# A group's projections moved ahead of the scans as seven half products each, and two scans woven beside the output projection

## The chip, the cores and the metric

The kernel runs on one core of a Trainium2 chip. The metric is the device time of one execution in microseconds (us), the median of three runs.

## The reference, cut to what matters

The trunk has two layers, a selective state space (SSD) layer and a pooling layer. 1,024 prompt tokens and 64 sample tokens (8 sequences of 8) go through it together, 1,088 columns in all. Only the first layer is touched here:

```python
zxbcdt = h @ w_in                       # h: normed, modulated x (1024 features)
z, xbc, dt_raw = ...                    # z: 2048, x: 2048, B, C: 8 groups of 128 each
conv = conv_b + sum(xp[:, k:k+L] * conv_w[k] for k in range(4))
xbc_act = silu(conv)                    # x, B and C of each of 8 groups
y, new_ssm = ssd_scan(xs, dt, A, B, C, ssm_prev)   # chunks of 128 tokens, state carried along
gated = (y + D * xs) * silu(z)          # then normed within each group of 256 channels
out = (gated * norm_g) @ w_out          # 2048 -> 1024, the output projection
x = x + (1 + gate) * out
```

The eight groups are independent until the output projection, which sums over all 2,048 gated channels.

## The kernel before, in words

All data are float32, and each number is split into a high and a low part so that a product takes three matrix multiplications (high by high, high by low, low by high: L168 to L170 in one helper, L922 to L924 in the other). TensorE (PE) does nearly all of the work; VectorE (DVE), ScalarE (ACT) and GpSimd (POOL) make the parts, evacuate the sums from PSUM and do the scans' elementwise work; SyncE (SP) issues the DMAs.

The first layer goes through these stages:

- **Front** (up to about 270 us): norm, modulation, and then eight *pairs* of weight tiles, named in the table `FRONT`. A pair computes two 128-column tiles of the projection at once by a scheme of seven half products in place of eight (`fast_pair`): products B11, B21, T2, T3, T1, T4, B22, each of 24 matmuls of 272 columns. Each product takes one or two PSUM buffers by tag, in the order mm mm, tr tr, y y, mm S, mm mm, tr tr, y y; there are two buffers of tags tr and y, so T4 can start only when B21's sums have been added up by DVE (`put`, L933), and B22 only when T2's have been. A pair of kind z gives two tiles of z, which go to DRAM. A pair ("b", g) gives B and C of group g and ("x", g) its two x tiles. These four tiles then pass the convolution, `conv_tile`: ACT L332, three DVE steps L334, ACT L337 (the sigmoid's half), DVE L338 and L340. The sums before the convolution and its accumulator lie in buffers called `raw`, of which there are three.
- **Scans** (about 270 to 791 us): for g from 0 to 6 the scan of group g is woven beside the four projection tiles of group g+1 (`proj_group`: four weight tiles of 72 matmuls of 364 or 360 columns, each followed by its convolution). `weave` takes one step of the scan and then some steps of the other work.
- **Transition and scan 7** (791 to 876 us): scan 7 has no projection left to stand beside, and is woven with part 0 of the output projection. That projection is done in four parts of four k (512 of the 2,048 gated channels); a part has 24 units of 12 matmuls. For each k, `op_stage` loads the gated tile `gr` from DRAM (and the norm factors `rs` for each two k), and `op_split` multiplies the two (DVE L679) and splits the result into `gh` (ACT L683) and `gl` (DVE L684). k = 0 to 3 are needed for part 0.
- **Rest of the output projection** (876 to about 1,030 us): the parts that are left, with the splits of the next part paced among their units (`op_paced`), then the pooling layer.

The order in which an engine gets its instructions is fixed when the kernel is built, by the order of the code and the buffers' priorities. An engine does its instructions in that order, and one that waits holds up all those behind it.

Of the kernel before, what the change touches and what calls it, by code (L numbers as in the profile page):

```python
# [7 lines left out]
F32 = mybir.dt.float32  # L8
# [6 lines left out]
P = 128  # L15
# [14 lines left out]
AE = 1  # L30
# [5 lines left out]
NSLOT_E = 4  # L36
FRONT = (("z", 2), ("z", 3), ("z", 4), ("z", 5), ("b", 0), ("z", 6), ("x", 0), ("z", 7))
WIDE = 1223
# [11 lines left out]
class Slots:  # L50
# [11 lines left out]
    def add_extra(self, pool, n):  # L62
        self.e = [f"e{i}" for i in range(n)]
        self.pools.update({t: (pool, TOK) for t in self.e})

    def get(self, name, dtype=F32, wide=False, short=False, extra=False):
        older = short and self.a and self.b and self.freed.get(self.b[0], 0) <= self.freed.get(self.a[0], 0)
        tag = (self.e if extra and self.e else self.b if self.b and (wide or older or not self.a) else self.a).pop(0)
        pool, w = self.pools[tag]
        self.n += 1  # L70
        t = pool.tile([P, w], dtype, tag=tag, name=f"{name}_{self.n}")
        v = t if wide else t[:, :TOK]
        self.used[id(v)] = (tag, v)
        return v

    def free(self, *ts):
        for t in ts:
            tag = self.used.pop(id(t))[0]
            {"s": self.a, "t": self.b, "e": self.e}[tag[0]].append(tag)
            self.count += 1  # L80
            self.freed[tag] = self.count


class Build:
    def __init__(self, tc, io):
        self.tc, self.nc, self.io = tc, tc.nc, io
        self.uid = 0

# [253 lines left out]
    def raw_tile(self):  # L342
        return self.gp.tile([P, 1115], F32, tag="raw", bufs=3, name=self.name("raw"))

# [119 lines left out]
    def scan_group(self, g, T):  # L464
# [160 lines left out]
        for c in range(8):  # L625
            Fn = front(c + 1)
            if c == 7:
                self.slots.free(B)
            back(c, F)
            F = Fn  # L630
            if c == 5:
                load_h0()
            if c == 6:
                load_z()
            if c == 7:
                zsc = sample_inter()
                self.slots.free(C)
            yield
        nc.sync.dma_start(self.io["hpT"][g], h.rearrange("p r q -> p (r q)"))
# [26 lines left out]
    def op_stage(self, src, k, short=False, rsd=None):  # L666

        if rsd and k % 2 == 0:
            self.rst = self.slots.get("rs", short=short)
            self.nc.sync.dma_start(self.rst, rsd[k // 2].rearrange("j n -> (j n)").unsqueeze(0).to_broadcast([P, TOK]))  # L670
        raw = self.slots.get("gr", short=short)
        self.nc.sync.dma_start(raw, src[k])
        return k, raw, self.rst if rsd else None
# [365 lines left out]
    def run(self):  # L1039
# [7 lines left out]
        items += [(io["win"][6 * g + {"b": 0, "x": 2, "z": 4}[kind] + i], 0) for kind, g in FRONT for i in range(2)]  # L1047
        for g in range(1, 8):
            for ii in range(4):
                items.append((io["win"][6 * g + ii], 8))  # L1050
                if (g, ii) in self.ada_plan:
                    items += self.ada_items(self.ada_plan[g, ii])
# [12 lines left out]
        with tc.tile_pool(name="cp", bufs=1) as self.cp, tc.tile_pool(name="wp", bufs=1) as self.wp, \  # L1065
# [7 lines left out]
            self.rsd = [dr.tile([4, 272], F32, tag=f"rsd{i}", name=f"rsd{i}") for i in range(8)]  # L1073
            self.zsd = [dr.tile([P, TOK], F32, tag=f"zsd{i}", name=f"zsd{i}") for i in range(16)]
            self.b12d = [dr.tile([P, HALF], F32, tag=f"b12d{i}", name=f"b12d{i}") for i in range(8)]
            self.x1d = [dr.tile([P, TOK], F32, tag=f"x1d{i}", name=f"x1d{i}") for i in range(8)]
            with tc.tile_pool(name="gp", bufs=1) as self.gp:
                with tc.tile_pool(name="ga", bufs=1) as self.tp:
                    self.slots.add_extra(self.tp, NSLOT_E)
                    self.setup()  # L1080
                    self.front()
                with tc.tile_pool(name="gs", bufs=1) as self.gs:
                    self.ssd_layer()
            with tc.tile_pool(name="gp2", bufs=1) as self.gp2:
# [135 lines left out]
    def front_pairs(self, ops, dt):  # L1220

        nc, sl = self.nc, self.slots
        self.fast_init(len(FRONT))
        G = None
        for n, (kind, g) in enumerate(FRONT):
# [3 lines left out]
            else:  # L1229
                G = G or self.proj_open(g)  # L1230
                ii = 2 * (kind == "x")
# [3 lines left out]
            def after(x):  # L1235
# [11 lines left out]
                if kind != "z" and x == "B22":  # L1247
                    for i in range(2):
                        self.proj_end(G, ii + i, ts[i])
                if n == 0 and x in ("B11", "B21"):  # L1250
                    next(ops)
# [11 lines left out]
        sl.free(*[self.T[4, k] for k in range(4)])  # L1263
        self.G = G

    def ssd_layer(self):
        nc, sl = self.nc, self.slots
        T, sc = self.G["out"], ()
        for g in range(7):
            G = self.proj_open(g + 1)  # L1270
            sc, pr = self.scan_group(g, T), self.late(self.proj_group(G), 1, sc)
            T = G["out"]
            if g < 6:
                self.weave(itertools.islice(sc, 11), pr, (1, 1, 1, 1, 1, 1, 1, 1, 1, 1, 2))
# [6 lines left out]
        for _ in itertools.chain(sc, pr):  # L1281
            pass
        for a in self.ada_late[:AE]:
            for _ in self.ada_do(a):
                pass
# [6 lines left out]
        for d in range(XA):  # L1292
            self.load_x(d)
        sc, fill = self.scan_group(7, T), self.op_units(0, acts, self.ada_late[AE:])
        self.weave(itertools.islice(sc, 10), fill, (1, 2, 2, 2, 2, 2, 2, 2, 2, 2), False)

        self.nxt = [split(stage(k)) for k in (4, 5)]
        self.weave(sc, fill, (2, 2, 2))
        self.free_acts(acts)

# [7 lines left out]
    def weave(self, main, fill, counts, drain=True):  # L1308

        i, md, fd = 0, False, False  # L1310
        while not (md and fd):
            if not md:
                md = next(main, 0) == 0
            if md and not drain:
                return
            for _ in range(99 if md else counts[min(i, len(counts) - 1)]):
                fd = fd or next(fill, 0) == 0
# [8 lines left out]

    def op_paced(self, l, acts, nxt):

        next(nxt)
        for i, ins in enumerate(self.op_units(l, acts)):  # L1330
            if i % 3 == 2:
# [20 lines left out]
    def ssd_out(self):  # L1352
        nc, sl, x = self.nc, self.slots, self.x
        sg = self.vec[:, V_SG:V_SG + 16]
        acts = self.nxt
        for _ in self.op_part_load(self.gyd, sg, (6, 8), acts, False, self.rsd):
            pass
        for i in (2, 3):
            nxt = []
            self.op_paced(0, acts, self.op_part_load(self.gyd, sg, PARTS[i], nxt, i == 3, self.rsd))  # L1360
            self.free_acts(acts)
            acts = nxt
        ss, rst = sl.get("ss"), sl.get("rst")
# [198 lines left out]
```

## Time and profile before

| what | us |
|---|---|
| median of three runs | 1685.69 |
| fastest and slowest of them | 1685.56, 1687.11 |
| time of the profiled execution | 1685.18 |
| its span, from first to last instruction | 1683.4 |
| PE busy within the span | 1649.9 |

The profiled execution is 0.5 us under the median, and 1.8 us of its time lie around the span. PE is busy for 98% of the span, DVE for 76%, ACT for 47%, POOL for 26%. "Busy" holds a matmul at half clock for as busy as one at full clock, so the granted clock has to be read beside it. Times below are counted from the start of the span.

### The profile page before, as it was taken

How to read it: one execution, taken by the hardware profiler on the slowest of the kernel's cores; microseconds unless marked ns; L12 is line 12 of the kernel's file. 1: busy time of each engine (PE TensorE's matmuls, PEld its weight loads, DVE VectorE, ACT ScalarE, POOL GpSimd, SP SyncE). 2: the span in 40 equal slices, each digit the busy share in tenths (PEclk: the TensorE clock that was granted, in tenths of full speed). 3: DMA queues.
4: the chain of work that ended last, by engine and by line, in shares of the span. 5: the costliest groups of instructions: out<-in, count | busy, mean ns of one | idle time of the engine just before them, and what ended most of it. 6: DMA issues, size and time to landing. Idle time of an engine off the chain costs nothing.

```text
span 1683.4 us, 30188 instructions
## 1 busy us (share of the span) xinstructions
PE 1649.9 (98%) x11771; PEld 1556.7 (92%) x11771; DVE 1274.0 (76%) x2182; ACT 785.5 (47%) x1539; POOL 446.0 (26%) x467
## 2 busy tenths in 40 slices
PE   8999999999999999999999999999999999999997
PEld 6899999889898888888889998999999999999997
DVE  6897688777778778788787647999999876555545
ACT  6544336767657676767442227533332343122123
POOL 0134440313122231222010022376666620000012
PEclk9999999999999999999999999999999999999998
DMA  8422225445354544445875132132333467411102
GB/s 336 164 89 104 78 80 207 146 145 182 108 171 121 167 127 141 141 123 182 285 247 192 43 116 79 67 125 97 111 110 110 138 250 305 155 52 51 38 26 106
DMA packets 111246, 232.03 MB, mean 138 GB/s; under 512 B 16864, under 2 KB 56960, under 8 KB 111104
## 3 DMA queue, kind: packets, MB, share of 16 engines
q1 hardware_dynamic: 111104, 230.10, 40.2%
q8 instruction: 93, 1.52, 0.4%
q14 instruction: 49, 0.40, 0.1%
HBM read 172.09 MB, written 57.98 MB: 137 GB/s over the span
## 4 chain that ended last, share of the span: by engine, by line
PE 34%; POOL 8%; issue 8%; DVE 5%; DMA 1%; ACT 1%; POOLq 0%; SPq 0%; ACTq 0%; DVEq 0%
PE mm L168 9%; PE mm L169 9%; PE mm L170 9%; POOL w L162 2%; PE st L924 1%; PE st L923 1%; PE st L922 1%; POOL sw L888 1%; POOL sw L887 1%; POOL npl L777 1%; POOL wr L892 1%; POOL npl L778 1%; DVE gl L684 1%; POOL sw L894 1%; PE y L550 0%
## 5 line engine op out<-in xcount | busy, mean ns | idle before, releaser
L168 PE MATMUL mm<-gh,wh 128*128 128x364 f32 (+3 forms) x768 | 254.8, 333 | 1.7 <-DVE x L703 1.3
L169 PE MATMUL mm<-gl,wh 128*128 128x364 f32 (+3 forms) x768 | 254.0, 331 | 2.2 <-DVE gl L684 2.2
L170 PE MATMUL mm<-gh,wl 128*128 128x364 f32 (+3 forms) x768 | 253.7, 331 | 0.0
L168 PE MATMUL mm<-hh,wh 128*128 128x364 f32 x720 | 248.4, 345 | 0.0
L169 PE MATMUL mm<-hl,wh 128*128 128x364 f32 x720 | 239.0, 332 | 0.0
L170 PE MATMUL mm<-hh,wl 128*128 128x364 f32 x720 | 237.6, 330 | 0.0
L703 DVE SCALAR_TENSOR_TENSOR x<-mm,gat,x 128x364 f32<-128x364 f32 (+3 forms) x192 | 108.9, 571 | 148.3 <-PE mm L170 147.9
L924 PE MATMUL st<-hh,w 128*128 128x272 f32 x704 | 203.2, 289 | 0.8 <-DVE w L162 0.8
L923 PE MATMUL st<-hl,w 128*128 128x272 f32 x704 | 203.1, 288 | 0.0
L922 PE MATMUL st<-hh,w 128*128 128x272 f32 x704 | 202.9, 288 | 0.0
L125 ACT ACTIVATE wh<-wr 128x1024 fp32r<-128x1024 f32 x73 | 77.2, 1057 | 224.6 <-PE mm L169 209.1
L924 PE MATMUL st<-t,w 128*128 128x272 f32 x528 | 152.4, 289 | 3.8 <-POOL w L162 2.9
L923 PE MATMUL st<-t,w 128*128 128x272 f32 x528 | 152.2, 288 | 0.7 <-DVE t L1190 0.7
L922 PE MATMUL st<-t,w 128*128 128x272 f32 x528 | 151.7, 287 | 0.0
L168 PEld LDWEIGHTS mm<-gh,wh 128*128 128x128 f32 x768 | 144.8, 189 | 5.4 <-DVE x L703 2.0
L169 PEld LDWEIGHTS mm<-gl,wh 128*128 128x128 f32 x768 | 145.4, 189 | 3.8 <-DVE gl L684 2.8
L170 PEld LDWEIGHTS mm<-gh,wl 128*128 128x128 f32 x768 | 145.5, 189 | 0.3 <-issue 0.2
L563 POOL TENSOR_TENSOR hd<-h,cd 128x256 f32<-128x256 f32 x56 | 67.1, 1198 | 282.4 <-DVE h L564 139.4
L334 DVE SCALAR_TENSOR_TENSOR raw<-raw,cwh,raw 128x1112 f32<-128x1112 f32 x96 | 134.3, 1399 | 9.8 <-ACT raw L332 9.1
L168 PEld LDWEIGHTS mm<-hh,wh 128*128 128x128 f32 x720 | 135.4, 188 | 5.5 <-ACT raw L376 1.6
L169 PEld LDWEIGHTS mm<-hl,wh 128*128 128x128 f32 x720 | 135.5, 188 | 4.6 <-issue 3.0
L170 PEld LDWEIGHTS mm<-hh,wl 128*128 128x128 f32 x720 | 135.3, 188 | 3.0 <-issue 2.9
(267 smaller groups left out, 4060.7 us busy)
## 6 DMA issues: line engine op xcount, KB each, us to landing
wr<-win SPq DMA_DIRECT2D x48, 512.0 KB, 4.8
acb<-acd SPq DMA_DIRECT2D x64, 256.0 KB, 3.9
wr<-pin SPq DMA_DIRECT2D x32, 512.0 KB, 3.6
x<-xT SPq DMA_DIRECT2D x16, 544.0 KB, 7.3
zsd<-z SPq DMA_DIRECT2D x16, 544.0 KB, 2.7
z<-zsd SPq DMA_DIRECT2D x16, 544.0 KB, 5.8
gyd<-xbc SPq DMA_DIRECT2D x16, 544.0 KB, 4.9
gr<-gyd SPq DMA_DIRECT2D x16, 544.0 KB, 4.9
```

What stands on the lines that cost most here:

```text
L125: self.nc.scalar.activation(hi[:, :nk, :], raw[:, :nk, :], AF.Copy)
L162: eng.tensor_tensor(out=lo, in0=src, in1=hi.bitcast(F32), op=ALU.subtract)
L168: nc.tensor.matmul(ps[:, :n], hi[:, k, :], ah[:, a:a + n], start=first, stop=False)
L169: nc.tensor.matmul(ps[:, :n], hi[:, k, :], al[:, a:a + n], start=False, stop=False)
L170: nc.tensor.matmul(ps[:, :n], lo[:, k, :], ah[:, a:a + n], start=False, stop=last)
L334: nc.vector.scalar_tensor_tensor(out=acc[:, :n], in0=raw[:, k:k + n], scalar=w[k], in1=acc[:, :n], op0=ALU.mult, op1=ALU.add)
L563: nc.gpsimd.tensor_tensor(out=hd, in0=h, in1=cd.unsqueeze(2).to_broadcast([P, 4, 64]), op=ALU.mult)
L684: nc.vector.scalar_tensor_tensor(out=lo, in0=raw, scalar=scl[:, k:k + 1], in1=hi.bitcast(F32), op0=ALU.mult, op1=ALU.subtract)
L703: ins = nc.vector.scalar_tensor_tensor(out=x[d][:, a:a + pn], in0=ps[:, :pn], scalar=self.gat[l][:, d, 8:9], in1=x[d][:, a:a + pn], op0=AL ...
L922: nc.tensor.matmul(ps[c][:, :QUART], hi[:, k], xh[:, t], start=(k == 0), stop=False)
L923: nc.tensor.matmul(ps[c][:, :QUART], hi[:, k], xl[:, t], start=False, stop=False)
L924: nc.tensor.matmul(ps[c][:, :QUART], lo[:, k], xh[:, t], start=False, stop=(k == 3))
```

## The change

Group 7's B, C and x are projected in the front, as two more pairs of seven half products, `("b", 7)` and `("x", 7)`. Their four tiles go through the convolution there, are stored to DRAM (`xbd`) and loaded again for scan 7. Scans 0 to 5 stand beside the projections of groups 1 to 6 as before; scans 6 and 7 follow each other (`last_scans`) beside two and a half parts of the output projection (`ssd_parts`), two units after a scan step and three after the next, in turn. The `raw` buffers get tags of their own, r0 to r2, and after the last convolution they are lent to `gr` and `rs`. Loading z within a scan moves from step 5 or 6 to step 7. Lines move by 4 in the part up to 1,000: L334 becomes L338, L338 and L340 become L342 and L344, L679 and L684 become L683 and L688, L933 becomes L937, L162 becomes L166.

```diff
-FRONT = (("z", 2), ("z", 3), ("z", 4), ("z", 5), ("b", 0), ("z", 6), ("x", 0), ("z", 7))
+FRONT = (("z", 2), ("z", 3), ("z", 4), ("b", 7), ("z", 5), ("x", 7), ("b", 0), ("z", 6), ("x", 0), ("z", 7))
...
+    def add_raw(self, pool):
+        self.e = [f"r{i}" for i in range(3)]
+        self.pools.update({t: (pool, 1115) for t in self.e})
...
     def raw_tile(self):
-        return self.gp.tile([P, 1115], F32, tag="raw", bufs=3, name=self.name("raw"))
+        self.nraw += 1
+        return self.gp.tile([P, 1115], F32, tag=f"r{self.nraw % 3}", name=self.name("raw"))
...
-            self.rst = self.slots.get("rs", short=short)
+            self.rst = self.slots.get("rs", short=short, extra=True)
...
-        raw = self.slots.get("gr", short=short)
+        raw = self.slots.get("gr", short=short, extra=True)
...
-        for g in range(1, 8):
+        for g in range(1, 7):
             for ii in range(4):
                 items.append((io["win"][6 * g + ii], 8))
...
                     for i in range(2):
                         self.proj_end(G, ii + i, ts[i])
+                        if g:
+                            nc.sync.dma_start(self.xbd[ii + i], G["out"][ii + i])
+                            sl.free(G["out"][ii + i])
...
-        for g in range(7):
+        for g in range(6):
             G = self.proj_open(g + 1)
             sc, pr = self.scan_group(g, T), self.late(self.proj_group(G), 1, sc)
...
+        sl.add_raw(self.gp)
...
-        sc, fill = self.scan_group(7, T), self.op_units(0, acts, self.ada_late[AE:])
-        self.weave(itertools.islice(sc, 10), fill, (1, 2, 2, 2, 2, 2, 2, 2, 2, 2), False)
-
-        self.nxt = [split(stage(k)) for k in (4, 5)]
-        self.weave(sc, fill, (2, 2, 2))
-        self.free_acts(acts)
+        self.fill = self.ssd_parts(acts)
+        self.weave(self.last_scans(T), self.fill, (2, 3), False)
+        assert len(sl.e) == 3
+
+    def last_scans(self, T):
+
+        yield from self.scan_group(6, T)
+        T = [self.slots.get("xbc") for _ in range(4)]
+        for i, t in enumerate(T):
+            self.nc.sync.dma_start(t, self.xbd[i])
+        yield from self.scan_group(7, T)
+        self.scanned = True
+
+    def ssd_parts(self, acts):
+
+        sg = self.vec[:, V_SG:V_SG + 16]
+        self.scanned = False
+        for p in range(3):
+            nxt = []
+            ld = self.op_part_load(self.gyd, sg, PARTS[p + 1], nxt, p == 2, self.rsd)
+            yield from self.op_paced(0, acts, ld, (11, 2, 13)[p], self.ada_late[AE:] if p == 0 else (), p == 2)
+            self.free_acts(acts)
+            acts = nxt
+        self.nxt = acts
```

The first place at which the order matters is DVE's queue behind the last convolutions ahead of a pair. Before, pair z6 follows b0: `raw_2154` and `raw_2157` are the tiles of b0, `raw_2392` and `raw_2403` the accumulators of their convolutions, and the puts of z6 write `z_2413` and `z_2414`.

```order
L334 SCALAR_TENSOR_TENSOR raw_2392<-raw_2154,cwh,raw_2392 128x1112 x2
L162 TENSOR_TENSOR w_2449<-sw_2291,w_2449 128x512
L334 SCALAR_TENSOR_TENSOR raw_2392<-raw_2154,cwh,raw_2392 128x1112
L933 TENSOR_TENSOR z_2413<-st_2452,u_2415 128x272
L933 TENSOR_TENSOR z_2413<-st_2453,u_2415 128x272
L933 TENSOR_TENSOR u_2415<-st_2489,u_2415 128x272
L338 SCALAR_TENSOR_TENSOR xbc_2391<-raw_2154,raw_2392 128x1024
L340 SCALAR_TENSOR_TENSOR xbc_2391<-raw_2154,raw_2392 128x64
```

In the changed kernel pair b0 follows x7. `raw_2419` and `raw_2422` are the tiles of x7, `raw_2657` and `raw_2669` their accumulators, and the first put of b0 writes `raw_2684`.

```order
L338 SCALAR_TENSOR_TENSOR raw_2657<-raw_2419,cwh,raw_2657 128x1112
L342 SCALAR_TENSOR_TENSOR xbc_2656<-raw_2419,raw_2657 128x1024
L344 SCALAR_TENSOR_TENSOR xbc_2656<-raw_2419,raw_2657 128x64
L166 TENSOR_TENSOR w_2788<-sw_2556,w_2788 128x512
L338 SCALAR_TENSOR_TENSOR raw_2669<-raw_2422,cwh,raw_2669 128x1112 x2
L166 TENSOR_TENSOR w_2824<-wr_2554,w_2824 128x512
L338 SCALAR_TENSOR_TENSOR raw_2669<-raw_2422,cwh,raw_2669 128x1112
L166 TENSOR_TENSOR w_2858<-wr_2554,w_2858 128x512
L342 SCALAR_TENSOR_TENSOR xbc_2668<-raw_2422,raw_2669 128x1024
L344 SCALAR_TENSOR_TENSOR xbc_2668<-raw_2422,raw_2669 128x64
L937 TENSOR_TENSOR raw_2684<-st_2727,u_2690 128x272
L937 TENSOR_TENSOR raw_2684<-st_2728,u_2690 128x272
```

The puts of the next pair stood between the steps of the convolutions before; now the first of them (of product B21) stands behind both convolutions, since b0's tiles take up `raw` buffers that these still use.

The second place is SP's queue at the transition. Before, the loads of `gr` for k = 2 and 3 (`gr_9324`, `gr_9326`) stand ahead of the last scan's state output and of the first x tiles.

```order
L661 DMA gyd_86<-xbc_8410 128x1088
L672 DMA gr_9324<-gyd_75 128x1088
L109 DMA wr_9375<-adaA 128x1024
L672 DMA gr_9326<-gyd_76 128x1088
L619 DMA hsT<-h_129_8919 128x1024
L1325 DMA x_9338<-xT 128x1088
```

In the changed kernel the same two loads (`gr_9007`, `gr_9009`) stand behind the factors' output `rsd_126`, the x tiles and the first weights of the output projection.

```order
L663 DMA rsd_126<-z_8768 4x272
L368 DMA ncT<-ncv_8107 128x108
L1355 DMA x_9024<-xT 128x1088
L1355 DMA x_9025<-xT 128x1088
L113 DMA wr_9060<-adaA 128x1024
L107 DMA wr_9062<-wout 128x2x512
L1355 DMA x_9022<-xT 128x1088
L676 DMA gr_9007<-gyd_75 128x1088
L676 DMA gr_9009<-gyd_76 128x1088
```

They go into two of the lent `raw` buffers, those of the last convolution, so they wait for its last DVE step (L344) where before they went into buffers that were free earlier.

## Rows read from the trace of the kernel before

**Rows 1.** The page's busy times, and the granted clock in 40 slices.

```profile
PE 1649.9 (98%) x11771; PEld 1556.7 (92%) x11771; DVE 1274.0 (76%) x2182; ACT 785.5 (47%) x1539; POOL 446.0 (26%) x467
...
PEclk9999999999999999999999999999999999999998
```

**Rows 2.** Windows by stage: scans 5 and 6, transition, scan 7, plain projection.

```profile
core 0: us, PE busy (x) PEld busy (x) DVE busy (x) ACT busy (x) POOL busy (x), PEclk, DMA share, GB/s
...
640.00:714.00 74.00, 73.22 (x530) 65.46 (x529) 58.20 (x97) 50.84 (x113) 18.19 (x27) 1.00 0.39 120
714.00:791.50 77.50, 76.71 (x549) 67.19 (x547) 63.73 (x101) 54.37 (x117) 18.66 (x27) 1.00 0.46 147
791.50:810.00 18.50, 15.08 (x81) 11.99 (x81) 15.60 (x20) 9.72 (x13) 0.33 (x2) 0.72 0.82 298
810.00:876.40 66.40, 66.40 (x552) 55.99 (x550) 53.93 (x118) 31.78 (x77) 11.04 (x9) 1.00 0.76 251
900.00:1024.00 124.00, 123.96 (x746) 123.43 (x745) 71.81 (x131) 32.56 (x42) 18.04 (x21) 1.00 0.27 93
```

**Rows 3.** Windows of three pairs of the front: b0, z6, x0.

```profile
182.42:203.49 21.07, 21.07 (x170) 21.07 (x169) 11.68 (x22) 5.55 (x10) 8.98 (x9) 1.00 0.28 101
203.49:224.56 21.07, 21.07 (x170) 21.07 (x169) 19.15 (x24) 10.55 (x16) 10.72 (x10) 1.00 0.15 51
224.56:247.24 22.68, 21.33 (x170) 21.12 (x169) 17.14 (x35) 6.71 (x14) 10.87 (x13) 1.00 0.29 98
```

**Rows 4.** Timeline of PE and POOL, pair x0: start, length, instruction, idle before and releaser.

```profile
241.40 0.39 PE L924 MATMUL st<-t,w 128*128 128x272 f32 x1 [1.35 <-POOL w L162]
...
225.01 0.10 POOL L354 MEMSET raw<- 128x3 f32 x1 [8.54 <-DVE xbc L340]
...
240.07 1.27 POOL L162 TENSOR_TENSOR w<-wr,w 128x512 fp32r<-128x512 f32 x1
```

**Rows 5.** Timeline of DVE in pair z6, behind pair b0.

```profile
203.69 0.51 DVE L933 TENSOR_TENSOR raw<-st,u 128x208 f32<-128x208 f32 x2 [1.04 <-PE st L924]
205.58 2.79 DVE L334 SCALAR_TENSOR_TENSOR raw<-raw,cwh,raw 128x1112 f32<-128x1112 f32 x2 [1.39 <-ACT raw L332]
...
210.00 2.41 DVE L334 SCALAR_TENSOR_TENSOR raw<-raw,cwh,raw 128x1112 f32<-128x1112 f32 x1
...
217.63 1.36 DVE L334 SCALAR_TENSOR_TENSOR raw<-raw,cwh,raw 128x1112 f32<-128x1112 f32 x1
...
224.66 0.22 DVE L340 SCALAR_TENSOR_TENSOR xbc<-raw,raw 128x64 f32<-128x64 f32 x1
```

**Rows 6.** Timeline of ACT in pair z6.

```profile
212.58 1.14 ACT L337 ACTIVATE raw<-raw 128x1112 f32<-128x1112 f32 x1 [2.14 <-DVE raw L334]
...
216.14 1.32 ACT L332 ACTIVATE raw<-raw,cwh 128x1112 f32<-128x1112 f32 x1 [1.26 <-DVE xbc L340]
```

**Rows 7.** Windows: two stretches at half clock, one with a long idle.

```profile
22.70:29.50 6.80, 5.17 (x19) 3.30 (x19) 5.85 (x11) 3.85 (x7) 0.00 (x0) 0.50 1.03 410
...
797.50:807.80 10.30, 8.01 (x25) 6.85 (x26) 9.47 (x12) 6.01 (x6) 0.00 (x0) 0.50 1.02 394
...
1044.00:1052.00 8.00, 5.99 (x35) 5.30 (x34) 6.32 (x21) 5.45 (x19) 5.06 (x15) 1.00 0.00 0
```

**Rows 8.** Timeline of PE: idles at the transition, and at 1,048 us.

```profile
796.79 0.46 PE L505 MATMUL tr<-xbc,xbc 128*128 128x128 f32 x2 [1.00 <-DVE scl L262]
...
799.24 0.67 PE L169 MATMUL mm<-gl,wh 128*128 128x364 f32 x1 [1.89 <-DVE gl L684]
...
1048.13 0.44 PE L168 MATMUL pl<-hh,wh 128*128 128x360 f32 x1 [1.99 <-ACT hh L309]
```

**Rows 9.** Timeline of DVE at the transition.

```profile
802.64 0.22 DVE L340 SCALAR_TENSOR_TENSOR xbc<-raw,raw 128x64 f32<-128x64 f32 x1
802.78 2.61 DVE L684 SCALAR_TENSOR_TENSOR gl<-gr,vec,gh 128x1088 fp32r<-128x1088 f32 x2
```

**Rows 10.** DMA issues of the gated tiles: count, size, median from issue to landing.

```profile
gr<-gyd SPq DMA_DIRECT2D x16, 544.0 KB, 4.9
```

More of the change, by code (lines that the diff above doesn't have):

```diff
@@ L78, in free @@
             tag = self.used.pop(id(t))[0]
-            {"s": self.a, "t": self.b, "e": self.e}[tag[0]].append(tag)
+            {"s": self.a, "t": self.b}.get(tag[0], self.e).append(tag)
             self.count += 1
@@ L86, in __init__ @@
         self.tc, self.nc, self.io = tc, tc.nc, io
-        self.uid = 0
+        self.uid = self.nraw = 0
     def name(self, s):
@@ L632, in scan_group @@
                 load_h0()
-            if c == 6:
-                load_z()
             if c == 7:
@@ L637, in scan_group @@
                 self.slots.free(C)
+                load_z()
             yield
@@ L1074, in run @@
             self.zsd = [dr.tile([P, TOK], F32, tag=f"zsd{i}", name=f"zsd{i}") for i in range(16)]
+            self.xbd = [dr.tile([P, TOK], F32, tag=f"xbd{i}", name=f"xbd{i}") for i in range(4)]
             self.b12d = [dr.tile([P, HALF], F32, tag=f"b12d{i}", name=f"b12d{i}") for i in range(8)]
@@ L1081, in run @@
                     self.front()
+                assert len(self.slots.e) == NSLOT_E
+                self.slots.e = []
                 with tc.tile_pool(name="gs", bufs=1) as self.gs:
                     self.ssd_layer()
+            self.slots.e = []
             with tc.tile_pool(name="gp2", bufs=1) as self.gp2:
@@ L1223, in front_pairs @@
         self.fast_init(len(FRONT))
-        G = None
+        Gs = {}
         for n, (kind, g) in enumerate(FRONT):
@@ L1229, in front_pairs @@
             else:
-                G = G or self.proj_open(g)
+                G = Gs.get(g) or Gs.setdefault(g, self.proj_open(g))
                 ii = 2 * (kind == "x")
@@ L1263, in front_pairs @@
         sl.free(*[self.T[4, k] for k in range(4)])
-        self.G = G
+        self.G = Gs[0]
     def ssd_layer(self):
@@ L1272, in ssd_layer @@
             T = G["out"]
-            if g < 6:
+            if g < 5:
                 self.weave(itertools.islice(sc, 11), pr, (1, 1, 1, 1, 1, 1, 1, 1, 1, 1, 2))
@@ L1315, in weave @@
                 return
-            for _ in range(99 if md else counts[min(i, len(counts) - 1)]):
+            for _ in range(99 if md else counts[i % len(counts)]):
                 fd = fd or next(fill, 0) == 0
@@ L1325, in load_x, with op_paced @@
         self.nc.sync.dma_start(self.x[d], self.io["xT"][d])
[L1327 to L1331, printed above, removed]
+    def op_paced(self, l, acts, nxt, start, ada=(), scanned=False):
+        for i, ins in enumerate(self.op_units(l, acts, ada)):
+            if i == start - 1:
+                assert self.scanned or not scanned
+                next(nxt)
+            if i >= start and (i - start) % 3 == 0:
                 with self.tc.issue_after(ins.ins):
                     next(nxt, None)
+            yield
         for _ in nxt:
@@ L1353, in ssd_out @@
         nc, sl, x = self.nc, self.slots, self.x
-        sg = self.vec[:, V_SG:V_SG + 16]
+        for _ in self.fill:
+            pass
         acts = self.nxt
[L1356 to L1362, printed above, removed]
         ss, rst = sl.get("ss"), sl.get("rst")
```

## The prediction

> **What bounds the kernel now.** I read the page first: PE is busy for 1649.9 of 1683.4 us at nearly full clock throughout [rows 1], so a gain has to take matmuls away or fill one of PE's few idles, and anything that makes PE wait is paid at once. Then the windows by stage [rows 2]. In the scans PE is busy to within 0.8 us of each 74 to 77.5 us, and in scan 7 it has no idle at all (66.40 of 66.40) while DVE is busy for 53.93, or 81%. The transition between the last projection and the output projection is the weak place: 18.5 us hold 15.08 of busy time, at a mean clock of 0.72. In plain projection 746 matmuls take 124.00 us, 0.166 us each. A pair of the front, 168 matmuls of 272 columns, takes 21.07 us when nothing disturbs it [rows 3], 0.1254 us each. Last I read the timelines of the places where the change puts something new: the pair behind a group's convolutions [rows 5, 6], the pair with POOL's wait [rows 4] and the transition [rows 8, 9].
>
> **Matmuls taken away.** Four projection tiles of 72 matmuls go: 288 x 0.1665 = 48.0 us. Two pairs come: 2 x 21.07 = 42.1 us. That is -5.9 us, and it is PE time, which nothing hides. Everything else that PE does stays in number. (The Trainium skill, "TensorE: Matmul & The Clock Gate", section "Back-to-back issue gap", gives columns/2.4 + 2.5 ns; an estimate by it is 115.8 ns for 272 columns, some 153.6 for 364 and 360, and a saving of 5.3 us. The rows are 8% above it in both sizes, and the sum goes by the rows.)
>
> **POOL's wait in a pair "x".** In pair x0 PE stands for 1.35 us, and the pair takes 22.68 instead of 21.07 us: +1.6 [rows 3, 4]. POOL's memset of a `raw` buffer waited 8.54 us for the convolution before it (L340), and the weight sums behind it on POOL came late, the last one, at 240.07, just ahead of PE's wait. Pair x7 comes two pairs behind b7, as x0 behind b0, with the same three buffers and the same queue on POOL: **+1.5** (0 to 3). Pair b7 follows z4 and finds free buffers, as b0 did before (21.07 us, [rows 3]): nothing.
>
> **Pair b0 directly behind x7.** This is the term that I trust most in sign. In DVE's queue the first put of b0 stands behind both convolutions of x7. What these take after a pair's end is on record for b0 before: the first L334 starts at 205.58, ACT's L337 at 212.58, ACT's L332 of the second tile waits for the end of the first until 216.14, its last L334s run from 217.63, and the last L340 starts at 224.66 [rows 5, 6]. Counted from the pair's end at 203.49 that is 21.4 us with the end of L340. Of this, some is not chain: one L334 took 2.41 us beside POOL's weight sums where another took 1.36 [rows 5], and about 3.5 us are the next pair's puts between the steps, which no longer stand there. Taking the puts, and the contention, out as far as the chain over ACT lets me, the end comes at 18.5. So the first put ends between +18.9 and +21.8. PE meanwhile has PSUM for B11, B21, T2, T3 and T1: five products of 24 x 0.1254 = 15.05 us. T4 needs a buffer of tag tr that this put frees. PE idles for 3.9 to 6.8 us; I take **+4.5**, nearer the lower end, since the puts are surely gone. Behind the put stand only short adds of b0 (some 0.4 us each), which T4's 3 us cover. Nothing could fill the idle, since PE's queue there is only this pair. (The Trainium skill, "SBUF — State Buffer", section "Who interferes with whom", has DVE and GpSimd share a pair of ports under an exclusive lock; the 2.41 against 1.36 us agrees, and it is a reason for the upper end.)
>
> **The clock after that idle.** Two stretches of before ran at a granted clock of 0.50, for 6.8 and 10.3 us, the second behind idles of 1.00 and 1.89 us close together; one single idle of 1.99 us left the clock at 1.00 [rows 7, 8]. An idle of 4.5 us is longer than each of these and longer than the sum of the first two, so I expect a drop. If 6.8 to 10.3 us run at half clock, and some 2 us of them fall into the idle itself, 4.8 to 8.3 us of work run at half speed, which loses half of it: 2.4 to 4.2. I take **+3.0** (0 to 4.2). (The Trainium skill, "TensorE: Matmul & The Clock Gate", section "Why this matters for your kernels", says to avoid long idles between bursts of matmuls lest the clock fall back; by that rule the 3 us belong in the sum as well.)
>
> **The transition.** Before, the loads of `gr` for k = 2 and 3 were done well ahead, and both `gl` were ready by 802.78 + 2.61 = 805.39 [rows 9]. Now they are issued only after the last L344. That one comes about 1 us earlier than the 802.64 + 0.22 of before [rows 9], since the two L679 stand behind it: about 801.9. A load of this kind takes 4.9 us [rows 10]: 806.8. Then L679, ACT's gh and DVE's gl in a row, 1.3 us each (half of 2.61, [rows 9]): 810.7 and 812 for the two, 6.6 us later than before. In between PE has the scan's own matmuls in its order; a chunk of a scan costs PE (76.71 - 48.0)/8 = 3.6 us [rows 2], of which I count about three quarters ahead of the units that wait: 2.6. Left: **+4.0**, with 0 (the scan covers it, or the low clock there, which was paid before as well, is over sooner) and 7 (the loads take half as long again, the DMA share being 1.02 there [rows 7]) as bounds.
>
> **From scan 6 to scan 7.** The four tiles from `xbd` are loaded when scan 6 frees its buffers; each is of the size of `gr`, 4.9 us [rows 10]. PE has five units there, 60 x 0.166 = 10 us [rows 2]. The loads land about 2.5 us ahead of need: **+0.5** (0 to 3).
>
> **Costed at nothing.** Two scans beside units: scan 7 beside part 0 shows no idle of PE with DVE at 81%. The new pacing adds some two splits to a scan of about 85 us, each 2.6 us (L684 1.3 [rows 9], and as much for L679), so DVE comes to some 87%, still under PE. The stores to `xbd` and loads move 2.2 MB each way while the DMA engines are at 0.15 to 0.29 in the front [rows 3]; the stores wait for nothing that PE needs. The z loads at step 7 are covered by the rest of the scan.
>
> **Sum.** -5.9 + 1.5 + 4.5 + 3.0 + 4.0 + 0.5 = +7.6. The profiled execution of 1685.18 becomes 1692.8; its median stands 0.5 above it: **1693 us**.
>
> **Rivals.**
> - *The stall is short.* If the convolutions of x7 end at +18.5 or sooner, PE idles for 3 us or less and the clock stays up, as after the 1.99 us [rows 8]; with 3 us less at the clock and 1.5 at the idle the sum is +3: 1688, no change that can be told. For it: the 1.99 us idle. Against it: the chain over ACT in [rows 6].
> - *The gain stays (the other side).* One mechanism: the late first put. If DVE works through the two convolutions within the 15.05 us that PE's five products last, the idle and the low clock both vanish, and if scan 6's matmuls cover k = 2 and 3 as they may, what is left is -5.9 + 1.5 + 0.5 = -3.9: 1682. It decides at a first put ending at +15 instead of +19; against it stands the measured +21.4 of [rows 5]. The transition could even gain, since a drop of the clock is already paid there before (10.3 us at half, about 5 us lost [rows 7]), and scan 6 has more filler beside it: then 1679 or so.
> - *The scans suffer.* Two scans beside split work put DVE at 87% for 170 us. If units that wait for a split or an evacuation in DVE's queue stand for 0.05 us each in 60 units and the hand-over costs its 3 us, that is +6 more: 1699. For it: every waiting gr holds up the scan's steps behind it on DVE. Against it: no idle in [rows 2] at 81%.
>
> **How the numbers follow.** A measurement tells 0.2% from no change here, 3.4 us. Chances: forecast 0.47; short stall 0.18; gain stays 0.22; scans suffer 0.13. The forecast by itself runs from 1689 to 1698 with the bounds of the stall and the transition. The range 1681 to 1702 leaves out the lower part of the gain and the far end of the last case. Faster by over 0.2% means under 1682.3, a part of the third case with its better transition and a little of the others: 0.21. Within 0.2% (to 1689.1): 0.20. Slower: 0.59.
>
> **What the changed profile would show.** Pairs b7 and x7 of 21.1 and 22.6 us; behind x7 in pair b0 an idle of PE of 4 to 6 us, released by DVE's put L937 into `raw`, ahead of T4, and PEclk 0.50 for some us after it; at the transition PE waiting for `gl` (L688) some us longer than before, with the `gr` loads issued after the last L344; the scans 6 and 7 without idle. The prediction is wrong if pair b0 shows no idle, if the clock stays at 1.00 after it, or if the transition is no longer than it was.

## The result, and the profile after

The changed kernel takes 1692.13 us (median of 5 runs, 1691.21 to 1693.65), the kernel before, beside it, 1686.55 us (5 runs, 1685.56 to 1688.04). The ratio is 1.0038, with a 95% interval of 1.0027 to 1.0049: slower by 0.38%, some 6 us. The forecast was 1693 in a range of 1681 to 1702.

First the page of the changed kernel, its busy times, beside [rows 1]. PE is busy for 1.8 us less than before, while the span has grown from 1683.4 to 1691.8 us: 288 matmuls gave way to 336 shorter ones (48 more in all), and idle time came.

```profile
span 1691.8 us, 30389 instructions
...
PE 1648.1 (97%) x11819; PEld 1553.8 (92%) x11819; DVE 1290.8 (76%) x2220; ACT 786.2 (46%) x1536; POOL 459.1 (27%) x479
```

Next the windows of the pairs b7, z5, x7, b0, z6 and x0, to be read beside [rows 3]: length, busy time of PE, PEld, DVE, ACT and POOL, the granted clock, the DMA share, GB/s.

```profile
162.23:183.31 21.08, 21.08 (x171) 21.08 (x169) 11.77 (x22) 5.56 (x10) 8.98 (x9) 1.00 0.28 99
183.31:204.38 21.07, 21.07 (x170) 21.07 (x169) 19.21 (x24) 10.57 (x16) 10.76 (x10) 1.00 0.21 78
204.38:226.88 22.50, 21.34 (x170) 21.12 (x169) 16.78 (x35) 6.72 (x14) 10.60 (x11) 1.00 0.35 124
226.88:257.17 30.29, 23.53 (x170) 23.34 (x169) 22.51 (x31) 9.59 (x13) 12.89 (x15) 0.89 0.21 74
257.17:278.25 21.08, 21.08 (x170) 21.08 (x169) 19.13 (x24) 10.44 (x16) 9.51 (x9) 1.00 0.16 52
278.25:300.84 22.59, 21.43 (x170) 21.16 (x169) 17.00 (x35) 6.93 (x15) 10.89 (x13) 1.00 0.30 99
```

Five of the six are what the same kinds of pair took before. Pair b0 takes 30.29 us where it took 21.07, and it is the only one whose clock is under 1.00. PE's waits from 80 to 325 us (waiting line, releaser, total, times, longest) say which wait it is:

```profile
PE st L926 <- DVE raw L937: 6.8, 1, 6.8
PE st L928 <- POOL w L166: 2.3, 2, 1.2
PE st L927 <- DVE t L1198: 0.7, 2, 0.3
```

One wait of 6.8 us for one put of DVE into a `raw` buffer. The timelines of DVE, ACT and PE in that pair (start, length, engine, instruction, and in brackets the idle before it and what ended it) show the chain, which answers to [rows 5, 6]:

```profile
228.97 2.79 DVE L338 SCALAR_TENSOR_TENSOR raw<-raw,cwh,raw 128x1112 f32<-128x1112 f32 x2 [1.39 <-ACT raw L336]
...
233.40 2.40 DVE L338 SCALAR_TENSOR_TENSOR raw<-raw,cwh,raw 128x1112 f32<-128x1112 f32 x1
237.08 2.22 DVE L342 SCALAR_TENSOR_TENSOR xbc<-raw,raw 128x1024 f32<-128x1024 f32 x1 [1.28 <-ACT raw L341]
...
240.96 2.79 DVE L338 SCALAR_TENSOR_TENSOR raw<-raw,cwh,raw 128x1112 f32<-128x1112 f32 x2 [0.93 <-ACT raw L336]
243.66 0.69 DVE L166 TENSOR_TENSOR w<-wr,w 128x512 fp32r<-128x512 f32 x1
244.26 1.38 DVE L338 SCALAR_TENSOR_TENSOR raw<-raw,cwh,raw 128x1112 f32<-128x1112 f32 x1
...
246.90 1.23 DVE L342 SCALAR_TENSOR_TENSOR xbc<-raw,raw 128x1024 f32<-128x1024 f32 x1 [0.66 <-ACT raw L341]
248.04 0.22 DVE L344 SCALAR_TENSOR_TENSOR xbc<-raw,raw 128x64 f32<-128x64 f32 x1
248.29 0.79 DVE L937 TENSOR_TENSOR raw<-st,u 128x272 f32<-128x272 f32 x2
...
239.53 1.32 ACT L336 ACTIVATE raw<-raw,cwh 128x1112 f32<-128x1112 f32 x1 [1.96 <-DVE xbc L344]
...
248.88 0.57 PE L926 MATMUL st<-t,w 128*128 128x272 f32 x1 [6.76 <-DVE raw L937]
```

The last L344 starts 21.2 us behind the start of the pair (248.04 against 226.88), the first put follows it at once (+21.4), and T4's first matmul follows the put. Two windows show what the idle did to the clock; the columns are as above:

```profile
241.90:248.90 7.00, 0.24 (x3) 0.06 (x2) 6.27 (x9) 1.76 (x2) 0.25 (x2) 0.86 0.08 34
...
248.88:253.70 4.82, 4.82 (x21) 4.82 (x22) 3.49 (x11) 0.00 (x0) 0.34 (x2) 0.50 0.28 116
```

A mean of 0.86 over the first means that the clock had fallen to half for about its last 2 us (0.14/0.50 x 7.0). Then 21 matmuls take 4.82 us instead of 21 x 0.1254 = 2.63: 2.2 us lost.

At the transition the loads of `gr` for k = 2 and 3 and the instructions around them are these (timelines of SP, DVE and PE), beside [rows 8, 9]:

```profile
782.01 0.80 SPq L676 DMA_DIRECT2D gr<-gyd  x2
...
781.72 0.22 DVE L344 SCALAR_TENSOR_TENSOR xbc<-raw,raw 128x64 f32<-128x64 f32 x1
...
790.70 1.35 DVE L688 SCALAR_TENSOR_TENSOR gl<-gr,vec,gh 128x1088 fp32r<-128x1088 f32 x1
...
789.10 0.80 PE L172 MATMUL mm<-gh,wh 128*128 128x364 f32 x3 [0.54 <-ACT gh L687]
...
790.58 0.67 PE L173 MATMUL mm<-gl,wh 128*128 128x364 f32 x1 [0.69 <-DVE gl L688]
```

Both loads are issued right behind the last L344, and the second `gl` is ready at 792.05, 10.1 us behind the end of that L344. Before it was 2.5 us behind it (805.39 against 802.86, [rows 9]). PE's waits from 760 to 900 us then total 7.5 us, where before three waits made 3.5:

```profile
PE mm L172 <- ACT gh L687: 2.2, 2, 1.7
PE mm L173 <- DVE gl L688: 2.1, 2, 1.4
PE y L555 <- DVE M L525: 1.2, 1, 1.2
PE tr L514 <- DMA xbc<-xbd: 0.6, 1, 0.6
PE tr L510 <- ACT Bt L531: 0.6, 1, 0.6
PE tr L514 <- DVE xbc L342: 0.4, 1, 0.4
PE am L247 <- DMA wr<-adaG: 0.4, 1, 0.4
```

Only 0.54 and 0.69 us of this are the waits for `gh` and `gl` of k = 2 and 3 (the PE lines above), which made 0.26 and 0.28 before. The other waits for `gh` and `gl` (1.71 and 1.37) stand ahead of the last L344, and three waits, 2.2 us together, are for tiles of scan 6 (M, Bt and xbc). (The lines of the scans moved by 5 and not by 4: L510 here is L505 in [rows 8].)

By stages, from the starts of the first and last matmul of each in the two traces (us); "scans" here is the stretch with group projections, "output" the stretch from the last of them to the last matmul of the output projection:

| stage | before | after | difference |
|---|---|---|---|
| start, to the first pair | 93.05 | 94.70 | +1.65 |
| front, all pairs | 175.15 | 227.09 | +51.94 |
| scans | 523.13 | 449.59 | -73.54 |
| output, with the scans in it | 235.53 | 264.12 | +28.59 |
| pooling layer | 646.38 | 645.96 | -0.42 |

The start is not touched by the change; over the kernels run here it takes between 92.7 and 94.8 us. The granted clock tells the two groups apart. In the changed kernel PE idles for 2.07 us ahead of 17.36 us, and the clock then stands at 0.50:

```profile
18.30:21.60 3.30, 3.30 (x16) 1.27 (x18) 0.16 (x1) 2.63 (x6) 0.00 (x0) 0.50 1.03 411
```

Before, it idles for 1.35 us there, and the same window has 1.00. All five kernels with the low clock there start their pairs at 94.3 to 94.8 us (this idle is 1.87 to 2.23 us in them), all six without it at 92.7 to 93.5 (0.50 to 1.35 us). So 1.65 of the 8.4 us by which the two profiled executions differ are of this one execution; the medians differ by 5.6.

### The profile page after: what moved, and what is told of

It reads as the page before. It is cut to its first block, busy times and chain, and to the rows that moved or that the text cites. A ratio compares the mean times of both kernels' runs of the same rounds, so it can differ in the third digit from the quotient of the medians.

```text
span 1691.8 us, 30389 instructions
## 1 busy us (share of the span) xinstructions
PE 1648.1 (97%) x11819; PEld 1553.8 (92%) x11819; DVE 1290.8 (76%) x2220; ACT 786.2 (46%) x1536; POOL 459.1 (27%) x479
## 4 chain that ended last, share of the span: by engine, by line
PE 65%; DVE 11%; issue 10%; POOL 10%; ACT 2%; DMA 2%; SPq 0%; POOLq 0%; ACTq 0%; DVEq 0%
PE mm L172 14%; PE mm L173 14%; PE mm L174 14%; PE st L928 3%; PE st L926 3%; PE st L927 3%; POOL w L166 2%; PE y L555 2%; PE S L562 2%; DVE raw L338 2%; PE y L559 1%; POOL sw L892 1%; PE am L247 1%; POOL sw L891 1%; PE tr L514 1%
## 5 line engine op out<-in xcount | busy, mean ns | idle before, releaser
L928 PE MATMUL st<-hh,w 128*128 128x272 f32 x768 | 221.6, 289 | 0.1
L927 PE MATMUL st<-hl,w 128*128 128x272 f32 x768 | 221.6, 288 | 0.0
L926 PE MATMUL st<-hh,w 128*128 128x272 f32 x768 | 221.4, 288 | 0.0
L172 PE MATMUL mm<-hh,wh 128*128 128x364 f32 (+1 forms) x624 | 215.3, 345 | 0.0
L173 PE MATMUL mm<-hl,wh 128*128 128x364 f32 (+1 forms) x624 | 207.1, 332 | 0.0
L174 PE MATMUL mm<-hh,wl 128*128 128x364 f32 (+1 forms) x624 | 205.8, 330 | 0.0
L926 PE MATMUL st<-t,w 128*128 128x272 f32 x576 | 166.7, 289 | 6.8 <-DVE raw L937 6.8
L928 PE MATMUL st<-t,w 128*128 128x272 f32 x576 | 167.3, 290 | 4.7 <-POOL w L166 3.9
L927 PE MATMUL st<-t,w 128*128 128x272 f32 x576 | 167.0, 290 | 0.7 <-DVE t L1198 0.7
L129 ACT ACTIVATE wh<-wr 128x1024 fp32r<-128x1024 f32 x69 | 73.0, 1058 | 185.6 <-PE mm L173 168.9
L338 DVE SCALAR_TENSOR_TENSOR raw<-raw,cwh,raw 128x1112 f32<-128x1112 f32 x96 | 137.7, 1435 | 13.1 <-ACT raw L336 12.5
L926 PEld LDWEIGHTS st<-hh,w 128*128 128x128 f32 x768 | 144.8, 189 | 0.4 <-issue 0.3
L928 PEld LDWEIGHTS st<-hh,w 128*128 128x128 f32 x768 | 144.4, 188 | 0.3 <-DVE w L166 0.3
L927 PEld LDWEIGHTS st<-hl,w 128*128 128x128 f32 x768 | 144.5, 188 | 0.0
```

Of the source, the lines that this page charges most:

```text
L129: self.nc.scalar.activation(hi[:, :nk, :], raw[:, :nk, :], AF.Copy)
L172: nc.tensor.matmul(ps[:, :n], hi[:, k, :], ah[:, a:a + n], start=first, stop=False)
L173: nc.tensor.matmul(ps[:, :n], hi[:, k, :], al[:, a:a + n], start=False, stop=False)
L174: nc.tensor.matmul(ps[:, :n], lo[:, k, :], ah[:, a:a + n], start=False, stop=last)
L338: nc.vector.scalar_tensor_tensor(out=acc[:, :n], in0=raw[:, k:k + n], scalar=w[k], in1=acc[:, :n], op0=ALU.mult, op1=ALU.add)
L926: nc.tensor.matmul(ps[c][:, :QUART], hi[:, k], xh[:, t], start=(k == 0), stop=False)
```

## Experiments

All ratios are to the kernel before, run beside each kernel on the same chip (its medians there: 1685.46, 1685.19 and 1685.24 us), with 95% intervals. The changed kernel itself stands at 1.0038 [1.0027, 1.0049].

**Another buffer for b0.** The counter of the `raw` tags is moved on by one ahead of pair b0 and set back behind the front:

```diff
                 ii = 2 * (kind == "x")
+                self.nraw += (kind, g) == ("b", 0)
                 ts = [self.proj_begin(G, ii + i) for i in range(2)]
...
         sl.free(*[self.T[4, k] for k in range(4)])
+        self.nraw += 2
         self.G = Gs[0]
```

> The two tiles of pair b0 get the raw buffers one further on, so that the first put of b0 waits for the first convolution of x7 only; nothing else changes. Theory (the idle in b0 is the wait of B21's sums for a buffer that the second convolution holds, and the low clock follows from it): the idle of 6.8 us and the half clock in pair b0 go, pair b0 takes 21 to 22 us instead of 30.3; since T3's and T1's sums still wait for the second convolution, 1 to 2.5 us of idle come at the start of z6. Net 6 to 8 us faster than the changed kernel, about 1685. Rival (DVE's total work behind x7 is the bound, whatever the order): the same work of DVE has to be done before T4 or before z6, so the wait moves and the time falls by under 3 us.

1687.7 us, ratio 1.0017 [1.0009, 1.0026]. The windows of pairs b0, z6 and x0 of this kernel:

```profile
226.88:249.60 22.72, 21.29 (x170) 21.07 (x168) 18.92 (x22) 10.10 (x14) 10.88 (x12) 1.00 0.21 74
249.60:271.90 22.30, 21.40 (x168) 21.22 (x169) 20.83 (x32) 8.45 (x13) 11.06 (x12) 1.00 0.21 74
271.90:295.70 23.80, 21.52 (x170) 21.13 (x169) 19.62 (x37) 7.98 (x16) 11.65 (x13) 1.00 0.29 94
```

The idle of 6.8 us and the half clock are gone by a choice of buffer alone. Three smaller waits stand in their place (1.5, 1.6 and 0.7 us for DVE's puts), as DVE still has the same work to do: the front takes 221.86 us, 5.2 less than the changed kernel, of the 9.2 by which b0 exceeded 21.07. The gain by the ratios, about 3.5 us, is under the 6 to 8 expected, and above the rival's 3 only just, less than the two intervals can tell apart; by the windows of the front it is the wait's place that mattered, and part of it moved. The rival had that part right.

**POOL's memsets given to DVE.**

```diff
-    def proj_begin(self, G, ii):
+    def proj_begin(self, G, ii, eng=None):
...
-        nc.gpsimd.memset(raw[:, 0:3], 0.0)
-        nc.gpsimd.tensor_copy(raw[:, 1027:1115].rearrange("p (b w) -> p b w", w=11)[:, :, 0:3], G["scv"][:, ii])
+        eng = eng or nc.gpsimd
+        eng.memset(raw[:, 0:3], 0.0)
+        eng.tensor_copy(raw[:, 1027:1115].rearrange("p (b w) -> p b w", w=11)[:, :, 0:3], G["scv"][:, ii])
...
-                ts = [self.proj_begin(G, ii + i) for i in range(2)]
+                ts = [self.proj_begin(G, ii + i, nc.vector) for i in range(2)]
```

> The memset and the copy that fill the pads of a raw buffer in the front are done by DVE instead of POOL. Theory (POOL's queue is held up by a memset that waits for a convolution, and the weight sums behind it come late): the 1.2 us idles in pairs x7 and x0 go, each pair falls from 22.5 to 21.1 us, 2.5 to 3 us faster than the changed kernel, about 1689.3; b0's idle stays within 0.5 us. Rival (the weight sums are late because their weights, or ACT's high parts, come late): the idles stay and the time stays within 1 us of 1692.

1691.82 us, ratio 1.0041 [1.0029, 1.0053]. Nothing moved: the same two waits are there, from 80 to 325 us:

```profile
PE st L927 <- DVE raw L938: 6.9, 1, 6.9
PE st L929 <- POOL w L166: 2.6, 2, 1.4
```

So the memset that waits 8.5 us on POOL [rows 4] was a bystander. In the changed kernel's pair x7 POOL's first weight sum waits for ACT's high part (3.12 us <-ACT w L164), a buffer is then freed late, SP issues the next weights at 211.02, and POOL waits 4.40 us for them. The same chain stood in the trace of before, in pair x0, behind the memset at 225.01 and with POOL free by then:

```profile
228.43 1.30 POOL L162 TENSOR_TENSOR w<-wr,w 128x512 fp32r<-128x512 f32 x1 [2.84 <-ACT w L160]
...
235.76 1.29 POOL L887 TENSOR_TENSOR sw<-wr 128x512 f32<-128x512 f32 x1 [4.58 <-DMA wr<-win]
```

That the chain over ACT and SP sets PE's wait is read from the traces; no run took it apart.

**The idle filled.** 40 matmuls that nobody needs ahead of T1 in pair b0:

```diff
...
+        if self.dummies and x == "T1":
+            for _ in range(self.dummies):
+                nc.tensor.matmul(ps[0][:, :QUART], hi[:, 0], self.X[x][0][0][:, :QUART], start=True, stop=True)
...
+            self.dummies = 40 * ((kind, g) == ("b", 0))
             self.fast_pair(*outs, after)
+            self.dummies = 0
```

> 40 matmuls that nobody needs (272 columns, 5.0 us) are put ahead of T1 in pair b0, into the buffer that T1 then starts afresh, so that PE's idle ahead of T4 shrinks from 6.8 to about 1.8 us while T4 cannot start earlier. It parts the idle from the clock. Theory (the half clock behind the idle costs some 2.3 us): the granted clock stays at 1.00 in pair b0, the pair takes 28 instead of 30.3 us, the time falls by 2 to 2.6 us to about 1689.8. Rival (the drop of the clock costs nothing that is not hidden, or comes from elsewhere): the time is the same, or up by some of the 5 us.

The profile shows the theory's side: pair b0, 40 matmuls of idle work included, takes 28.2 us instead of 30.3, with the clock at 1.00 throughout, and T4 waits for the same put as before:

```profile
225.60:253.80 28.20, 26.44 (x210) 26.25 (x210) 22.21 (x31) 9.58 (x13) 13.03 (x15) 1.00 0.23 80
```

```profile
247.75 0.36 PE L929 MATMUL st<-t,w 128*128 128x272 f32 x1 [1.76 <-DVE raw L940]
```

So of the 9.2 us by which pair b0 exceeds an undisturbed one, some 2.1 are the low clock behind the idle, and the rest is the idle. The low clock goes with the idle in the other traces too: the two other kernels that keep the idle (6.9 us each, in the experiments just before and just behind this one) have 0.50 behind it as well, and the two in which another buffer takes it away have 1.00 throughout. The timed runs don't show the 2.1 us: 1692.0 us, ratio 1.0041 [1.0028, 1.0054], which stands against the window; with runs of one kernel 3 us apart, five of them can't decide on 2 us.

**Ordinary buffers for k = 2 and 3.**

```diff
-        st = [stage(2), stage(3)]
+        st = [self.op_stage(self.gyd, k, False, self.rsd, False) for k in (2, 3)]
...
-    def op_stage(self, src, k, short=False, rsd=None):
+    def op_stage(self, src, k, short=False, rsd=None, extra=True):
...
-            self.rst = self.slots.get("rs", short=short, extra=True)
+            self.rst = self.slots.get("rs", short=short, extra=extra)
...
-        raw = self.slots.get("gr", short=short, extra=True)
+        raw = self.slots.get("gr", short=short, extra=extra)
```

> The staged tiles and factors of k = 2 and 3 get ordinary buffers as before the change, not those of the last convolution; all later stages keep the lent ones. Theory (k = 2 and 3 come late because their buffers do): both loads are issued ahead of the last convolution, gl for k = 3 is ready some 5 us earlier against the last L344, the idles behind the first units (1.15, 0.54, 0.69 us) shrink, and the time falls by 2.5 to 4 us to about 1689. Rival (the transition is bound by the last convolution and by ACT and DVE work that is there in any case): under 1 us.

1689.02 us, ratio 1.0020 [1.0011, 1.0029]: about 3 us under the changed kernel. The last L344 and the two `gl` of this kernel, and PE's waits from 760 to 900 us:

```profile
780.62 0.22 DVE L344 SCALAR_TENSOR_TENSOR xbc<-raw,raw 128x64 f32<-128x64 f32 x1
780.75 2.61 DVE L688 SCALAR_TENSOR_TENSOR gl<-gr,vec,gh 128x1088 fp32r<-128x1088 f32 x2
```

```profile
PE mm L173 <- DVE gl L688: 2.2, 2, 1.9
PE tr L510 <- DVE scl L266: 1.0, 1, 1.0
PE am L247 <- DMA wr<-adaG: 0.8, 1, 0.8
PE tr L514 <- DMA xbc<-xbd: 0.6, 1, 0.6
PE mm L172 <- ACT gh L687: 0.3, 1, 0.3
```

Both `gl` follow the last L344 at once, as before the change, and the waits are those of before (2.2, 1.0, 0.3) with 1.4 us of new DMA waits. The stretch from the last projection to the end of the output projection falls from 264.12 to 259.79 us. The lent buffers cost 4.3 us here, of which 2.7 are idle of PE; the rest goes with the clock, which stood at 0.50 for 6.8 us of this stretch and for 10.2 in the changed kernel.

**Both edits.**

> Both edits that helped together: b0's tiles in the raw buffers one further on, and ordinary buffers for k = 2 and 3. Theory (two separate waits, in the front and at the transition): the gains add, 5.2 us in the front and 3 to 4.5 us at the transition by the windows, 7 to 9 us under the changed kernel, about 1684, so 1 to 2 us under the kernel before. Rival (the waits share a cause, or the noise of the timed runs made one of them): 1687 to 1689, as each alone.

1683.07 us, ratio 0.9989 [0.9980, 0.9998]: 2 us under the kernel before, with an interval that only just leaves out no change, and 8 under the changed one. By the ratios the gains add, the waits being in two places: another buffer for b0 makes 3.5 us alone and 5.2 beside the ordinary buffers, these 3.0 alone and 4.7 beside the other buffer. The traces bear this out for the front (222.24 us, 4.7 under the 226.95 with ordinary buffers alone), less so for the transition: the stretch from the last projection to the end of the output projection is 260.25 us, only 1.1 under the 261.35 of the kernel with b0's other buffer alone, which lies under the 264.12 of the changed kernel without an edit there. Over all kernels run here that stretch takes 261.4 to 264.7 us in the five with lent buffers for k = 2 and 3, and 259.0 to 260.3 in the five with ordinary ones: the sign holds throughout, the size does not. This is the fastest version found.

**Another order of the front,** z2 z3 z4 b7 z5 x7 z6 b0 z7 x0, alone and with the ordinary buffers.

```diff
-FRONT = (("z", 2), ("z", 3), ("z", 4), ("b", 7), ("z", 5), ("x", 7), ("b", 0), ("z", 6), ("x", 0), ("z", 7))
+FRONT = (("z", 2), ("z", 3), ("z", 4), ("b", 7), ("z", 5), ("x", 7), ("z", 6), ("b", 0), ("z", 7), ("x", 0))
```

> The changed kernel with another order of the front alone: z2 z3 z4 b7 z5 x7 z6 b0 z7 x0, so that a z pair stands behind x7 and behind b0. Theory (only the pair directly behind a convolution that needs its raw buffers pays the long wait): no idle over 2 us in any pair, 1.4 us each in x7, b0 and x0, the front about 219.5 instead of 227.1 us; but x0 is last, and its two convolutions (21 us behind its end) hold up the first scan's x, which the first projection tile covers by 12 us only, so 0 to 6 us come back at the first scan. Net 2 to 8 us faster. Rival (any order with four group pairs among six z pairs pays the same): same time.

> The same order of the front with ordinary buffers for k = 2 and 3: a further 3 to 4.5 us under the order alone, 1681 to 1687, by the theory that the two places are independent.

The order alone gives 1696.55 us, ratio 1.0066 [1.0052, 1.0080], slower than the changed kernel. The front does what was expected: 217.95 instead of 227.09 us, no wait for a put. But scan 0 waits for the convolutions of x0, which stands last; PE's waits from 80 to 345 us:

```profile
PE tr L514 <- DVE xbc L342: 8.9, 2, 6.0
...
```

The scans take 461.99 us instead of 449.59: 12.4 us. PE's idle makes 8.0 of them, this wait above all, and the clock some 4.4: two stretches of work behind the two waits ran at half clock (the columns are as above).

```profile
323.33:326.36 3.03, 3.03 (x11) 3.03 (x12) 1.41 (x3) 2.82 (x7) 0.00 (x0) 0.50 0.50 189
...
334.29:340.02 5.73, 5.73 (x24) 4.58 (x24) 4.14 (x10) 4.85 (x12) 1.11 (x7) 0.50 0.01 1
```

The expectation had 0 to 6 us for this place, and was wrong in size and so in sign. With the ordinary buffers it is 1692.34 us, ratio 1.0038 [1.0025, 1.0050], 4.2 us less than without, as those were worth above and as was expected (by the traces 264.16 to 259.89 us, with 10.2 us at half clock in both); the 1681 to 1687 rested on the gain that the order was to bring.

**x7 last,** z2 z3 z4 b0 z5 x0 z6 b7 z7 x7, with ordinary buffers for k = 2 and 3, and the same with the `raw` counter moved on by one behind the front.

> Front in the order z2 z3 z4 b0 z5 x0 z6 b7 z7 x7 with ordinary buffers for k = 2 and 3. x7 is last and needed by scan 7 only. Theory (e6 lost its gain because scan 0 waited for the convolutions of x0, the pair that stood last): no pair waits for over 2 us, scan 0 starts without an idle on its x, front about 218 us. What can wait is the sums of the first projection tile beside scan 0, whose raw buffer the second convolution of x7 holds until 21 us behind the front: 0 to 8 us. 1678 to 1687. Rival (the last pair's DVE work holds up scan 0 whatever group it belongs to): 1690 or more, like e7.

> As e9, with the raw buffers of the group projections one further on, so that the first projection tile takes the one that the first convolution of x7 frees. Theory: the idle of e9 beside scan 0, if there is one, shrinks to under 2 us, and the time is 1678 to 1682, 4 to 7 us under the kernel before. Rival (DVE's work, 10 us of convolution at the start of scan 0, is the bound): the same as e9.

1690.5 us, ratio 1.0025 [1.0016, 1.0034], and 1687.35 us, ratio 1.0011 [1.0002, 1.0020]. Better than with x0 last, since no scan waits long for the last pair's tiles any more, but neither the 1678 to 1687 nor the 1678 to 1682 expected. PE's waits of the second from 80 to 420 us:

```profile
PE st L926 <- DVE z L937: 3.1, 2, 2.2
...
PE y L555 <- DVE M L525: 1.7, 1, 1.7
```

Pair z7 takes 24.6 us (3.1 us of waits for DVE), so the front is 221.97 us and not 218; the stretch of the scans is 453.16, 3.6 more than in the changed kernel, all of it in scan 0. The wait of 1.7 us for DVE there, against 0.8 in the changed kernel, is 0.9 of that; where the rest goes is not shown. In each order run here DVE's convolution work shows up somewhere. Between the first and the second kernel a buffer again makes 3 us by the medians, 3.4 in the stretch of the scans. In the first, scan 0 has four waits, 3.5 us together, and the clock stands at 0.50 from 338.5 us on; in the second it stays at 1.00:

```profile
338.50:345.30 6.80, 6.80 (x29) 4.60 (x29) 6.78 (x11) 4.45 (x13) 1.00 (x4) 0.50 0.54 181
```

## Why the prediction was right, step by step

- **Matmuls taken away, -5.9.** Right as far as it can be read: b7 took 21.08 us, and x7 22.50 with the wait of the next term; 73.5 us of group projection and scan left the stretch of the scans. PE's busy time fell by 1.8 and not by 5.9, since matmuls at half clock count for longer: 2.2 us in b0, and some 1.7 in the 3.4 us at half clock that the start of this execution has more.
- **A wait of POOL's weight sums in x7, +1.5.** It took 1.43 (22.50 - 21.07). Right in size and wrong in cause: the memset named for it was taken from POOL, and the wait stayed. [rows 4] has the memset 15 us ahead of the weight sum that came late, and the waits of POOL between the two, for ACT and for a load, had not been read.
- **The idle in pair b0, +4.5 (3.9 to 6.8).** The place, the releaser and the waiting product were right; the size was 6.8, the upper end. The step that was mis-sized is "taking the puts, and the contention, out". In the changed kernel the second convolution ends as late behind the pair's start as in [rows 5] (21.4 us): a step of the first tile still runs slowed beside POOL (2.40 against 1.38 us), ACT's first step of the second tile still waits for the end of the first, and a weight part of 0.69 us stands where a put stood. In the places of the other puts DVE is idle and waits for ACT (1.28, 0.93 and 0.66 us in the rows above): they had filled time in which the chain ran on ACT. Leaving out work beside a chain had not shortened the chain. (The Trainium skill, "SBUF — State Buffer", section "Who interferes with whom", has DVE and GpSimd share one pair of ports under an exclusive lock; 2.40 against 1.38 us agrees with it, and no run here took POOL's weight sums away.)
- **The clock behind it, +3.0 (0 to 4.2).** It fell, for 2 us of the idle and 4.8 us of work, and cost 2.2 us by the rows. Without the long idle it stayed at 1.00.
- **The transition, +4.0 (0 to 7).** Right: the loads are issued right behind the last L344, and taking the lent buffers away again gives back 4.3 us in that stretch, 3.0 in the timed ratio. The second `gl` came at 10.1 us behind the L344, as the sum had it (812 against 801.9), and PE's waits grew by the 4.0 forecast (3.5 to 7.5). They were the forecast ones in part only: PE's waits for `gh` and `gl` of k = 2 and 3 grew by 0.7, and most of the rest is waits of scan 6, which was to have no idle, and of DMAs. So the size is partly luck. The 4.3 us stand in two pairs of kernels that differ by this alone (the other is the other order's), and a third pair has 1.1.
- **From scan 6 to scan 7, +0.5.** One wait of 0.6 us for a tile from `xbd`. The working was loose: a load of 4.9 us against 10 us of units leaves 5 us and not 2.5.
- **Two scans beside split work, nothing.** From 800 to 950 us PE's waits list nothing but two DMAs (0.6 and 0.4 us), so the rival of suffering scans didn't come behind the transition.
- **The sum, +7.6,** is 5.6 by the medians and 8.4 by the profiled executions, 1.65 of these at the untouched start. The front came out 0.8 above its terms, and the scans and the output together about 1.5 below theirs (-73.54 + 28.59 = -44.95 against -48.0 + 4.5). Pair b0 alone exceeded its two terms by 1.7 (9.2 against 7.5), so errors of both signs met, and that 1692.13 lies within 1 us of 1693 is partly luck: the kernel before ran at 1686.55 beside it and not at 1685.69. The rival of the other side needed the first put to end at +15 us; it began at +21.4. It was reachable by the choice of buffers, though: with another one for b0 and ordinary stage buffers the kernel is faster than before, by 2 us of the 3.9 that the rival had.

## What to carry to other kernels

A pair of work moved ahead is worth the matmul time that it saves only if the pools of buffers behind it are free. Here a gain of 5.9 us was turned into a loss by two allocations, each of which put a producer behind the end of a chain on other engines, and each of which was eased by taking another buffer; with both, 2 of the 5.9 us were left as a gain. When such a wait is costed, take the chain as measured and do not shorten it by the work that leaves its side, unless that work was on the chain. And where a long piece of work on DVE follows a stage, ask who stands behind it in every order: the wait moved from b0 to scan 0 and to z7 as the order was changed, and cost between 3 and 12 us there.

## What was not expected of the hardware

A wait of 6.8 us lowered the clock for only about 6.8 us in all, of which 2 lay in the wait, so that the price was 2.2 us; three or four waits of 0.7 to 1.8 us in neighbouring pairs left it at 1.00. Shorter waits were not safe, though. PE's idle of 1.99 us in the pooling layer that [rows 7, 8] show at 1,048 us, with the clock at 1.00, is in every kernel here (2.00 us in one); in six of the eleven profiled executions a stretch of some 3.4 us at 0.50 came behind it (1,049.2 to 1,052.5 us in the kernel with another buffer for b0). In the first kernel with x7 last, three idles of 0.26, 1.32 and 0.46 us close together stood ahead of the 6.8 us at 0.50 shown above. The prediction's reading, that one idle of 1.99 us leaves the clock up, was one outcome of two. The start of the kernel, before any of the changed work, took between 92.7 and 94.8 us over the executions profiled here, with or without such a stretch, more than some of the terms that were to be told apart.
